# Finishing the last 128 rows of a prefix sum in blocks of 32 rows, with TensorE weighing columns directly

## The chip, the cores and the metric

One NeuronCore of a Trainium2 chip. The metric is the device time of one execution in microseconds. The profile's span (first to last instruction) is some 1.7 us shorter than that time. "Clock" is the share of full speed that the throttle granted TensorE.

## The reference

```python
def setup_inputs():
    B, H, W = 4, 4224, 4224
    return {"x": np.random.randn(B, H, W).astype(np.float32)}

def reference(x):
    ps = np.cumsum(np.cumsum(x, axis=1), axis=2)
    diag = np.diagonal(ps, axis1=1, axis2=2)
    return np.cumsum(diag, axis=1).astype(np.float32)
```

Every output place needs the sum of x over a growing square, so all 285 MB of x must be read once, and the work on it is sums of rows, sums of columns and running sums along 4224 places.

## The kernel before: the parts that matter here

It reads x in strips of 768 rows, cast to bf16 by the DMA, and sums columns on TensorE and rows on ScalarE and VectorE. Apart from a small set-up step at the start, only the end of the last batch is touched by the change. There the last 384 rows come as an upper part (two blocks of 128 rows, `part_a`) and the last 128 rows (`part_b`), each in pieces of columns. The row sums of each are weighted and added to the last 384 output places.

```python
acuts = [(1536, N - HC), (0, 1536)]              # upper blocks, two pieces of columns
bcuts = [(2432, TB), (640, 2432), (0, 640)]      # last 128 rows, three pieces
... # loads on the gpsimd queue; the other places are finished by two scans
fold_in(fold_a, part_a, c0, cp, 256)             # TensorE folds part of the columns
for h in range(2):
    act_sum(asum[:, h, 3:4], part_a[:, h, cp:c1])    # ScalarE sums the others
row_sums(asum[:, :, 4], fold_a)
row_sums(arows, asum)
shares = [(768, 512), (768, 512), (0, 320)]
for i, ((c0, c1), (wp, wa)) in enumerate(zip(bcuts, shares)):
    fold_in(fold_b, part_b, c0, c0 + wp, 256, start=i == 0)
    act_sum(tsum[:, n : n + 1], part_b[:, c0 + wp : c0 + wp + wa])
    if i == 2:
        row_sums(tsum[:, n + 2 : n + 3], fold_b)
    row_sums(tsum[:, n + 1 : n + 2], part_b[:, c0 + wp + wa : c1])
    n += 2
    ... # after piece 0: the products of arows into fin_b and fin_a
row_sums(ttot, tsum)                             # one total per row
matmul(fin_b, ttot, weights[:, 0:P])             # weights: row r counts for places >= r
for fin, c0, c1 in ((fin_a, 0, 2 * P), (fin_b, 2 * P, GW)):
    nc.vector.tensor_add(out=yl[:, c0:c1], in0=fin, in1=c12[0:1, 1, c0:c1])
    nc.sync.dma_start(out=out[b, T0 + c0 : T0 + c1].unsqueeze(0), in_=yl[:, c0:c1])
```

## Time and profile before

| | before |
|---|---|
| time, median of the first 3 runs | 669.03 us (668.8 to 669.93) |
| span of the trace | 667.0 us |
| DMA engines busy | 90% or more in 39 of 40 slices |
| first use of the second upper piece, on ScalarE | 658.53 us |
| end of the last sums | 664.08 us |
| end of the last addition | 665.05 us |

The prediction below shows the profile's lines for these. Each line of the order of instructions gives the start and the length in us, the engine, the source line, the operation, and what it writes and reads. A bracket at the end is the idle time before it and what ended it. In the table of stretches, the columns are busy time (and count) of each engine, then the clock, the DMA share and GB/s.

### The profile page before, as it was taken

How to read it: one execution, taken by the hardware profiler on the slowest of the kernel's cores; microseconds unless marked ns; L12 is line 12 of the kernel's file. 1: busy time of each engine (PE TensorE's matmuls, PEld its weight loads, DVE VectorE, ACT ScalarE, POOL GpSimd, SP SyncE). 2: the span in 40 equal slices, each digit the busy share in tenths (PEclk: the TensorE clock that was granted, in tenths of full speed). 3: DMA queues.
4: the chain of work that ended last, by engine and by line, in shares of the span. 5: the costliest groups of instructions: out<-in, count | busy, mean ns of one | idle time of the engine just before them, and what ended most of it. 6: DMA issues, size and time to landing. Idle time of an engine off the chain costs nothing.

```text
span 667.0 us, 2828 instructions
## 1 busy us (share of the span) xinstructions
PE 215.1 (32%) x967; PEld 97.2 (15%) x967; DVE 336.3 (50%) x376; ACT 140.1 (21%) x225; POOL 27.0 (4%) x56
## 2 busy tenths in 40 slices
PE   0071522403118254140321633504032254250426
PEld 0030211101003022010110311201011122120202
DVE  2043617366924351745883415266398241635687
ACT  0001120406300103040630020304063002030436
POOL 5000000000000000000000000000000000001000
PEclk9995857666558586665655957567565586765758
DMA  9999999999999999999999999999999999999997
GB/s 203 219 219 219 218 219 219 217 217 216 208 215 219 219 219 217 216 219 219 219 219 215 216 211 217 220 219 216 216 216 219 220 215 218 216 215 219 216 207 144
DMA packets 7384, 143.25 MB, mean 215 GB/s; under 512 B 669, under 2 KB 842, under 8 KB 1866
## 3 DMA queue, kind: packets, MB, share of 16 engines
q0 software_dynamic: 7008, 142.47, 99.7%
q1 hardware_dynamic: 362, 0.61, 0.3%
q8 instruction: 7, 0.11, 0.1%
q14 instruction: 7, 0.06, 0.0%
HBM read 285.47 MB, written 0.07 MB: 428 GB/s over the span
## 4 chain that ended last, share of the span: by engine, by line
another core or an unknown queue 42%; DVE 25%; PE 23%; DMA 5%; issue 4%; DVEq 0%; POOLq 0%
PE d L198 23%; DVE acc L215 17%; DVE mu L218 7%; DMA strip<-in_x_dram 5%; PE fold L198 1%; DVE pu L215 0%; DVE c L397 0%; DVE c L218 0%; DVE tsum L215 0%; DVE acc L301 0%; DVE acc L304 0%; PE carry_ps L198 0%; DVE rows L331 0%; DVEq L218 0%
## 5 line engine op out<-in xcount | busy, mean ns | idle before, releaser
L218 DVE SCALAR_TENSOR_TENSOR mu<-strip,um 128x768 bf16<-128x768 bf16 (+1 forms) x129 | 110.7, 908 | 314.4 <-DMA strip<-in_x_dram 222.3
L198 PE MATMUL d<-strip,sel 128*11 128x384 bf16 x603 | 140.0, 406 | 344.4 <-DMA strip<-in_x_dram 344.4
L210 ACT ACTIVATE dump<-strip 128x416 bf16<-128x416 bf16 (+8 forms) x112 | 128.4, 1146 | 523.2 <-DMA strip<-in_x_dram 520.2
L215 DVE TENSOR_REDUCE acc<-strip 128x6 f32<-128x4608 bf16 (+6 forms) x23 | 195.9, 8518 | 0.0
L198 PEld LDWEIGHTS <-sel 128*11 128x11 bf16 x849 | 86.1, 101 | 526.3 <-issue 488.4
L198 PE MATMUL d<-mu,sel 128*11 128x384 bf16 x243 | 59.7, 355 | 67.5 <-DVE mu L218 67.4
L75 POOL DMA_DIRECT2D strip<-in_x_dram x24 | 16.5, 687 | 555.5 <-DVE acc L215 414.5
L210 ACT ACTIVATION_READ_ACCUMULATOR dump<-strip 128x1 f32 x112 | 20.9, 186 | 0.0
L218 DVE DVE_READ_ACCUMULATOR mu<-strip,um 128x1 f32 x129 | 10.6, 82 | 0.0
L198 PE MATMUL d<-ident,rows 128*11 128x128 f32 x24 | 5.2, 378 | 16.5 <-DVE rows L340 16.5
L198 PE MATMUL fold<-strip,ident_h 128*128 128x480 bf16 (+1 forms) x14 | 4.3, 458 | 8.4 <-DMA strip<-in_x_dram 8.4
L198 PE MATMUL d<-halves,rows 128*11 128x64 f32 x48 | 5.7, 304 | 0.0
L198 PEld LDWEIGHTS d<-halves,rows 128*11 128x11 f32 x48 | 5.1, 136 | 2.1 <-issue 2.1
L198 PEld LDWEIGHTS d<-ident,rows 128*11 128x11 f32 x24 | 2.6, 118 | 18.2 <-DVE rows L340 11.5
L215 DVE TENSOR_REDUCE pu<-d 11x1 f32<-11x384 f32 x4 | 2.2, 546 | 5.5 <-PE d L198 5.5
L397 DVE TENSOR_TENSOR_SCAN c<-ones_row,carry,c 11x384 f32<-11x384 f32 x4 | 4.0, 1006 | 0.1
L397 DVE TENSOR_TENSOR_SCAN c<-ones_row,carry,d 11x384 f32<-11x384 f32 x4 | 4.0, 1001 | 0.1
L198 PEld LDWEIGHTS <-ident_h 128*128 128x128 bf16 x20 | 2.2, 112 | 12.2 <-issue 11.8
L215 DVE TENSOR_REDUCE parts<-strip 128x3 f32<-128x3072 bf16 x1 | 3.4, 3350 | 0.0
L198 PE MATMUL d<-hmu,sel 128*11 128x384 bf16 (+2 forms) x3 | 0.7, 286 | 6.7 <-DVE hmu L218 6.7
L372 POOL DMA_DIRECT2D strip<-in_x_dram x2 | 1.4, 716 | 29.2 <-DVE acc L215 29.2
L215 DVE TENSOR_REDUCE tsum<-strip 128x1 f32<-128x384 bf16 (+2 forms) x3 | 1.7, 568 | 0.9 <-DMA strip<-in_x_dram 0.9
(78 smaller groups left out, 36.0 us busy)
## 6 DMA issues: line engine op xcount, KB each, us to landing
strip<-in_x_dram POOLq DMA_DIRECT2D x19, 6336.0 KB, 69.6
strip<-in_x_dram POOLq DMA_DIRECT2D x5, 3168.0 KB, 55.3
strip<-in_x_dram POOLq DMA_DIRECT2D x1, 1080.0 KB, 45.3
strip<-in_x_dram POOLq DMA_DIRECT2D x1, 768.0 KB, 48.2
head<-in_x_dram SPq DMA_DIRECT2D x1, 528.0 KB, 3.9
strip<-in_x_dram POOLq DMA_DIRECT2D x1, 448.0 KB, 51.1
strip<-in_x_dram POOLq DMA_DIRECT2D x1, 416.0 KB, 49.5
strip<-in_x_dram POOLq DMA_DIRECT2D x1, 160.0 KB, 51.4
```

What stands on the lines that cost most here:

```text
L75: nc.gpsimd.dma_start(out=o, in_=x[b, r0 : r0 + f * P, :].rearrange("(p f) w -> p f w", f=f))
L198: nc.tensor.matmul(o, lhsT=lhsT, rhs=rhs, start=start, stop=False, skip_group_check=True)
L210: nc.scalar.activation(out=dump[:, :w], in_=src, func=ACT.Copy, accum_out=acc)
L215: nc.vector.reduce_sum(out=acc, in_=src, axis=AX.X)
L218: nc.vector.scalar_tensor_tensor(out=o, in0=i, scalar=1.0, in1=m, op0=ALU.mult, op1=ALU.mult, accum_out=acc,)
L372: nc.gpsimd.dma_start(out=part_a[:, :, c0:c1], in_=src_a[:, :, c0:c1])
L397: nc.vector.tensor_tensor_scan(out=c12[:, i, :], data0=ones_row, data1=src, initial=carry[:, i : i + 1], op0=ALU.mult, op1=ALU.add,)
```

## The change

Its intent: after the last byte has landed, do less in series. The last 128 rows come as four blocks of 32 rows, and each row is spread over four partitions (128 partitions per block), the last block in two pieces. Blocks 0 and half of 1 are multiplied by TensorE with the place weights (`weights4`, each row's weight repeated four times). Their columns then only need adding up, which a product with a column of ones does. ScalarE and VectorE sum the rest, and every partial sum goes through its own product at once instead of through a total. The last 32 rows reach only the last 32 places, so these are finished apart from the others.

```diff
+    matmul(w4_ps, quarter, weights[:R, :P], start=True)      # set-up; R = 32
+    weights4 ... weights4_h ... ones_col ...
-            bcuts = [(2432, TB), (640, 2432), (0, 640)]
+            for sb, c0, c1 in ((0, 0, CB), (1, 0, CB), (2, 0, CB), (3, 0, bcut), (3, bcut, CB)):
+                r0 = TB + sb * R                                # CB = 1024, bcut = 640
+                nc.gpsimd.dma_start(out=part_b[:, sb, c0:c1],
+                    in_=x[b, r0 : r0 + R, :TB].rearrange("r (k c) -> r k c", k=4)[:, :, c0:c1])
-            fold_in(fold_a, part_a, c0, cp, 256, start=True)
+            fold_in(fold_a, part_a, c0, cp, P, start=True)
...
-        ttot = last.tile([P, 1], FP32, name="ttot")
-        row_sums(ttot, tsum)
-        matmul(fin_b, ttot, weights[:, 0:P])
+        for sb, cp in ((0, CB), (1, c1a)):                     # c1a = CB // 2
+            for c in range(0, cp, P):
+                matmul(by_ps[:, sb * R :], part_b[:, sb, c : c + P],
+                    weights4_h[:, : P - sb * R], start=sb == 0 and c == 0)
+        act_sum(bsum[:, 0:1], part_b[:, 1, c1a:])
+        nc.scalar.copy(out=by, in_=by_ps)
+        fins = ((fin_a, 0, M0), (fin_m, M0, E0), (fin_e, E0, GW))   # 256, 96, 32 places
+        ... # products of arows, of the diagonal, of bsum, and of ones_col with by
+        finish(fin_a, 0, M0)
+        act_sum(bsum[:, 1:2], part_b[:, 2, : CB // 2])
+        row_sums(bsum[:, 2:3], part_b[:, 2, CB // 2 :])
+        for k in (1, 2):
+            weigh(bsum[:, k : k + 1], weights4, M0 + 2 * R, fins)
+        for k, (c0, cm, c1) in enumerate(((0, 320, bcut), (bcut, bcut + 128, CB))):
+            act_sum(esum[:, 2 * k : 2 * k + 1], part_b[:, 3, c0:cm])
+            row_sums(esum[:, 2 * k + 1 : 2 * k + 2], part_b[:, 3, cm:c1])
+        for k in range(4):
+            weigh(esum[:, k : k + 1], weights4, E0, fins)       # only fin_e is reached
+        finish(fin_m, M0, E0)                                   # then out[.. : T0 + E0]
+        finish(fin_e, E0, GW)                                   # then the last 32 places
```

More of the change, by code (lines that the diff above doesn't have):

```diff
@@ L192 @@
     )
+    R = P // 4
+    quarter = consts.tile([R, P], FP32, name="quarter")
+    nc.gpsimd.memset(quarter, 1.0)
+    for base, step in ((0, 1), (3, -1)):
+        nc.gpsimd.affine_select(
+            out=quarter,
+            in_=quarter,
+            compare_op=ALU.is_ge,
+            fill=0.0,
+            base=base,
+            pattern=[[step, P]],
+            channel_multiplier=-4 * step,
+        )
     ident_h = consts.tile([P, P], BF16, name="ident_h")
@@ L200, in matmul @@
         )
+    w4_ps = psum_s.tile([P, P], FP32, name="fold")
+    matmul(w4_ps, quarter, weights[:R, :P], start=True)
+    weights4 = consts.tile([P, P], FP32, name="weights4")
+    nc.vector.tensor_copy(out=weights4, in_=w4_ps)
+    weights4_h = consts.tile([P, P], BF16, name="weights4_h")
+    nc.vector.tensor_copy(out=weights4_h, in_=w4_ps)
+    ones_col = consts.tile([P, 1], FP32, name="ones_col")
+    nc.vector.memset(ones_col, 1.0)
     def fold_in(o, src, c0, c1, w, start=False):
@@ L242 @@
     asum = last.tile([P, 2, 5], FP32, name="asum")
-    tsum = last.tile([P, 8], FP32, name="tsum")
+    dtot = last.tile([P, 1], FP32, name="dtot")
     hs = last.tile([P, 3], FP32, name="hs")
@@ L320 @@
                 masked(hmu[:, 2, :P], diag_b, um1[:, :P], hu[:, 2:3])
-                nc.vector.tensor_sub(
-                    out=tsum[:, 0:1], in0=hs[:, 2:3], in1=hu[:, 2:3]
-                )
+                nc.vector.tensor_sub(out=dtot, in0=hs[:, 2:3], in1=hu[:, 2:3])
                 for h in range(3):
@@ L368 @@
             part_a = strip[:, 0:2]
-            part_b = strip[:, 2]
+            part_b = strip[:, 2, :TB].rearrange("p (s c) -> p s c", s=4)
             acuts = [(1536, N - HC), (0, 1536)]
@@ L372 @@
                 nc.gpsimd.dma_start(out=part_a[:, :, c0:c1], in_=src_a[:, :, c0:c1])
-            bcuts = [(2432, TB), (640, 2432), (0, 640)]
-            for c0, c1 in bcuts:
-                nc.gpsimd.dma_start(out=part_b[:, c0:c1], in_=x[b, TB:N, c0:c1])
-            fold_a = psum_s.tile([P, 2, 256], FP32, name="fold_a")
+            CB = TB // 4
+            bcut = 640
+            for sb, c0, c1 in (
+                (0, 0, CB),
+                (1, 0, CB),
+                (2, 0, CB),
+                (3, 0, bcut),
+                (3, bcut, CB),
+            ):
+                r0 = TB + sb * R
+                nc.gpsimd.dma_start(
+                    out=part_b[:, sb, c0:c1],
+                    in_=x[b, r0 : r0 + R, :TB].rearrange("r (k c) -> r k c", k=4)[
+                        :, :, c0:c1
+                    ],
+                )
+            fold_a = psum_s.tile([P, 2, P], FP32, name="fold_a")
             c0, c1 = acuts[0]
             cp, ca = c0 + 768, c0 + 768 + 1152
-            fold_in(fold_a, part_a, c0, cp, 256, start=True)
+            fold_in(fold_a, part_a, c0, cp, P, start=True)
             for h in range(2):
@@ L415 @@
         cp = c0 + 768
-        fold_in(fold_a, part_a, c0, cp, 256)
+        fold_in(fold_a, part_a, c0, cp, P)
         for h in range(2):
@@ L421, with weigh, finish @@
         row_sums(arows, asum)
-        fold_b = psum_s.tile([P, 256], FP32, name="fold")
-        fin_a = psum_s.tile([1, 2 * P], FP32, name="fin_a")
-        fin_b = psum_s.tile([1, P], FP32, name="fin_b")
-        shares = [(768, 512), (768, 512), (0, 320)]
-        n = 1
-        for i, ((c0, c1), (wp, wa)) in enumerate(zip(bcuts, shares)):
-            fold_in(fold_b, part_b, c0, c0 + wp, 256, start=i == 0)
-            act_sum(tsum[:, n : n + 1], part_b[:, c0 + wp : c0 + wp + wa])
-            if i == 2:
-                row_sums(tsum[:, n + 2 : n + 3], fold_b)
-            row_sums(tsum[:, n + 1 : n + 2], part_b[:, c0 + wp + wa : c1])
-            n += 2
-            if i == 0:
-                matmul(fin_b, arows[:, 0:1], weights[:, 2 * P : GW], start=True)
-                matmul(fin_b, arows[:, 1:2], weights[:, P : 2 * P])
-                matmul(fin_a, arows[:, 0:1], weights[:, 0 : 2 * P], start=True)
-                matmul(fin_a[:, P : 2 * P], arows[:, 1:2], weights[:, 0:P])
-        ttot = last.tile([P, 1], FP32, name="ttot")
-        row_sums(ttot, tsum)
-        matmul(fin_b, ttot, weights[:, 0:P])
-        yl = last.tile([1, GW], FP32, name="yl")
-        for fin, c0, c1 in ((fin_a, 0, 2 * P), (fin_b, 2 * P, GW)):
+        M0 = 2 * P
+        E0 = GW - R
+        fin_a = psum_s.tile([1, M0], FP32, name="fin_a")
+        fin_m = psum_s.tile([1, E0 - M0], FP32, name="fin_m")
+        fin_e = psum_s.tile([1, R], FP32, name="fin_e")
+        yl = last.tile([1, GW], FP32, name="yl")
+        def weigh(rows, w, r0, fins, start=False):
+            for fin, f0, f1 in fins:
+                g0 = max(f0, r0)
+                if g0 < f1:
+                    matmul(
+                        fin[:, g0 - f0 :], rows, w[:, g0 - r0 : f1 - r0], start=start
+                    )
+        def finish(fin, c0, c1):
             nc.vector.tensor_add(
@@ L448 @@
             )
-            nc.sync.dma_start(
-                out=out[b, T0 + c0 : T0 + c1].unsqueeze(0), in_=yl[:, c0:c1]
-            )
+        by_ps = psum_s.tile([P, P], FP32, name="fold")
+        c1a = CB // 2
+        for sb, cp in ((0, CB), (1, c1a)):
+            for c in range(0, cp, P):
+                matmul(
+                    by_ps[:, sb * R :],
+                    part_b[:, sb, c : c + P],
+                    weights4_h[:, : P - sb * R],
+                    start=sb == 0 and c == 0,
+                )
+        bsum = last.tile([P, 3], FP32, name="bsum")
+        act_sum(bsum[:, 0:1], part_b[:, 1, c1a:])
+        by = last.tile([P, P], FP32, name="by")
+        nc.scalar.copy(out=by, in_=by_ps)
+        fins = ((fin_a, 0, M0), (fin_m, M0, E0), (fin_e, E0, GW))
+        weigh(arows[:, 0:1], weights, 0, fins[:1], start=True)
+        weigh(arows[:, 1:2], weights, P, fins[:1])
+        weigh(arows[:, 0:1], weights, 0, fins[1:], start=True)
+        weigh(arows[:, 1:2], weights, P, fins[1:])
+        weigh(dtot, weights, M0, fins)
+        weigh(bsum[:, 0:1], weights4, M0 + R, fins)
+        weigh(ones_col, by, M0, fins)
+        finish(fin_a, 0, M0)
[3 more added lines that the diff above has]
+            weigh(bsum[:, k : k + 1], weights4, M0 + 2 * R, fins)
+        esum = last.tile([P, 4], FP32, name="esum")
+        for k, (c0, cm, c1) in enumerate(((0, 320, bcut), (bcut, bcut + 128, CB))):
[4 more added lines that the diff above has]
+        finish(fin_m, M0, E0)
+        nc.sync.dma_start(
+            out=out[b, T0 : T0 + E0].unsqueeze(0), in_=yl[:, :E0]
+        )
+        finish(fin_e, E0, GW)
+        nc.sync.dma_start(out=out[b, T0 + E0 : N].unsqueeze(0), in_=yl[:, E0:])
 _INS = ['x']
```

## The prediction

> **What bounds the kernel now.** I read the page's strip of 40 slices first, then the queues, then the stretches of the tail one by one, and at last the order of instructions in the final 4 us. The slices and queues:
>
> ```profile
> DVE  2043617366924351745883415266398241635687
> PEclk9995857666558586665655957567565586765758
> DMA  9999999999999999999999999999999999999997
> GB/s 203 219 219 219 218 219 219 217 217 216 208 215 219 219 219 217 216 219 219 219 219 215 216 211 217 220 219 216 216 216 219 220 215 218 216 215 219 216 207 144
> ...
> q0 software_dynamic: 7008, 142.47, 99.7%
> ```
>
> The 16 DMA engines are 90% busy or more in 39 of 40 slices, at 215 to 220 GB/s (bytes as written in bf16; twice that is read). No compute engine is above 50% of the span. So the kernel is as long as reading x takes, plus a head of about 1 us and a tail after the last bytes. The change alters neither bytes nor the order of the large loads; it works only on the tail. How long is that tail? Stretches of the last microseconds (columns: stretch, its length, PE, weight loads, DVE, ACT, POOL, then clock, DMA share, GB/s):
>
> ```profile
> 656.50:658.50 2.00, 1.17 (x10) 0.48 (x9) 1.34 (x5) 0.90 (x2) 0.00 (x0) 1.00 1.07 211
> 658.50:660.50 2.00, 0.81 (x4) 0.29 (x4) 1.96 (x3) 1.87 (x4) 0.00 (x0) 1.00 1.07 211
> 660.50:662.60 2.10, 1.71 (x11) 0.85 (x11) 1.08 (x3) 0.72 (x2) 0.00 (x0) 1.00 0.63 116
> 662.60:663.50 0.90, 0.50 (x4) 0.23 (x3) 0.88 (x2) 0.72 (x2) 0.00 (x0) 1.00 0.04 7
> 663.50:665.30 1.80, 0.38 (x2) 0.09 (x2) 1.29 (x5) 0.56 (x2) 0.00 (x0) 1.00 0.00 0
> 665.30:667.00 1.70, 0.00 (x0) 0.00 (x0) 0.00 (x0) 0.00 (x0) 0.00 (x0) 0.66 0.00 1
> ```
>
> Transfers run full until about 661, thin out as the engines finish unevenly, and are over at about 663.3. From 663.5 to 665.3 only compute is left, then 1.7 us in which only the output's write is under way. The order of work in that end (start, duration, engine):
>
> ```profile
> 662.62 0.69 DVE L215 TENSOR_REDUCE tsum<-strip 128x1 f32<-128x512 bf16 x1 [0.94 <-DMA strip<-in_x_dram]
> ...
> 663.22 0.41 DVE L215 TENSOR_REDUCE tsum<-fold 128x1 f32<-128x256 f32 x1
> 663.51 0.47 ACT L210 ACTIVATE dump<-strip 128x320 bf16<-128x320 bf16 x1
> 663.55 0.47 DVE L215 TENSOR_REDUCE tsum<-strip 128x1 f32<-128x320 bf16 x1
> 663.89 0.19 ACT L210 ACTIVATION_READ_ACCUMULATOR dump<-strip 128x1 f32 x1
> 664.13 0.16 DVE L215 TENSOR_REDUCE ttot<-tsum 128x1 f32<-128x8 f32 x1
> 664.21 0.40 DVE L446 TENSOR_TENSOR yl<-fin_a,c 1x256 f32<-1x256 f32 x1
> 664.35 0.09 PEld L198 LDWEIGHTS fin_b<-weights,ttot 128*1 128x1 f32 x2 [1.50 <-DVE ttot L215]
> 664.35 0.38 PE L198 MATMUL fin_b<-weights,ttot 128*1 128x128 f32 x2 [1.22 <-DVE ttot L215]
> 664.64 0.66 SPq L449 DMA_DIRECT2D out_dram<-yl  x2
> 664.77 0.28 DVE L446 TENSOR_TENSOR yl<-fin_b,c 1x128 f32<-1x128 f32 x1 [0.16 <-PE fin_b L198]
> ```
>
> ScalarE begins the third piece at 663.51, 0.08 us after it was free, so I put that piece's landing at 663.47. The pieces before it were first used at 660.49 (416 KB) and 662.62 (448 KB), so the three land 2.03, 2.13 and 0.85 us apart, counting from the upper block at 658.49. After the landing: sums until 664.02, total until 664.29, matmul until 664.73, addition until 665.05, write until 667.0. That is 3.5 us, of which 1.6 us is compute. Only those 1.6 us, a quarter of one per cent, are on offer.
>
> **What the Trainium skill says.** [...] last addition done at 665.05, end at 667.0, 1.95 us, which the change cannot shorten. (2) "VectorE: DVE Perf Modes", section "The perf-mode tier table", allows tensor_reduce only the 1x mode in every type. The trace agrees: 686 ns for 512 columns and 474 for 320 give 1.10 ns a column, so 256 columns are about 0.40 us. (3) "ScalarE: Activation LUTs", section "What ACT_TABLE_LOAD costs", gives 186 ns + 0.833 ns a column with immediate operands; the trace has 629 ns for 512 and 469 for 320, the same slope. The next section lists copy as filler in every table set, so the new ScalarE copy should load no table; no run yet shows it. (4) "TensorE: Matmul & The Clock Gate", section "Back-to-back issue gap", has about 81 ns per pair of weight load and 128-column matmul in a full stream. The trace has no such bf16 pair; its 256-column ones with fresh weights start some 0.15 us apart (three in 0.49 us, the last 0.27 long, so two gaps of 0.11; I take 0.12 for 128).
>
> **The change part by part.**
>
> *Setup.* A memset and two selects on POOL after `weights` (10.28 to 10.79), each 0.1 to 0.2 us as its 11x11 selects show; one fp32 matmul; two copies and a memset on DVE, which now waits for POOL until about 12 us before sums that used to end at 8.8. The first strip lands at 34.6 us. About 20 us of slack: cost 0.
>
> *Loads.* The same 2 MB of x, as 256, 256, 256, 160 and 96 KB in bf16 instead of 416, 448 and 160. POOL issues them at 611 at about 0.6 us each, 50 us ahead: two more issues cost 0. On the queue, the first two old pieces ran at 205 to 210 KB per us, so 160 KB should have taken 0.77 us and took 0.85: some 0.08 us extra for a short piece. With two more pieces the last byte's signal comes about 0.13 us later, at 663.6. Landings: 659.75, 661.05, 662.3, 663.1, 663.6.
>
> *Upper blocks.* The fold of 768 columns by 256 becomes one by 128: six matmuls of 256 elements instead of three of 512, perhaps 0.2 us more on PE while it waits for DVE anyway, and the reduction of the fold falls from 0.66 to about 0.41 us (256 elements). `arows` is ready near 660.9 instead of 661.22. Not on the final path.
>
> *Blocks 0 and 1.* Eight plus four weighted matmuls replace the folds: 8 x 0.12 = 1.0 us inside the wait for block 1, then 4 x 0.12, done at about 661.65. ScalarE sums half of block 1 (0.75 us with its read) and copies the 128x128 product (about 0.3 us by the slope above) by 662.1. TensorE then owes fin_a (0.64 us between starts in the trace) and small fp32 pairs. From the trace a pass of 128 columns takes 0.107 us and passes of 1 or 2 columns start 0.02 us apart, so 96 columns cost 0.08 and 32 about 0.03: the two upper blocks 4 x 0.11 = 0.44, diagonal 0.22, block 1 0.16, product 0.22, block 2 0.22; with fin_a 1.9 us, from 661.65 to 663.55. That still precedes the last sums.
>
> *Last block.* ScalarE: 512 columns of block 2 from 662.3, 320 of piece one from 663.1 (0.60 to the next), 128 of piece two from 663.7, read at 664.1. VectorE: addition of fin_a 0.40 until 662.7, 512 columns until 663.3, 320 until 663.65, then 256 columns (0.40) until 664.0. The step `ttot` (0.16 plus 0.11 around it) is gone: each partial sum goes to PE itself. After 664.1: two pairs of 32 columns, about 0.16 us latency, ready at 664.4; addition of 32 places 0.19 (402 ns for 256, 279 for 128, 0.96 ns a place) until 664.65. Addition of fin_m (0.25) goes before it, in PE's shadow. The first output (352 places) is issued near 664.2 for 0.23 us, so SyncE is free for the second.
>
> *Sum on the path after the landing*: sums to 664.1 against 664.02 (+0.08, of which the landing is 0.13), total -0.27, matmul -0.14, addition -0.09: 664.65 against 665.05, so **-0.4 us**. Then the same 1.95 us. 669.03 - 0.4 = **668.6 us**.
>
> **The rivals.**
>
> 1. *TensorE becomes the bound.* It now has over 40 small fp32 passes in order behind block 1. If a pass costs 0.1 us whatever its width, as the weight loads' own 0.08 us hints, the list ends about 1.5 us later, near 665, and the last four esum products wait behind it: about +0.5 us, 669.5. Against it: the carry matmuls' starts 0.02 us apart. This is the rival I fear most.
> 2. *The loads get slower.* Five pieces in runs of 4 KB instead of 6.6 or 7 KB. If each piece cost 0.3 us extra, or the new row order spread unevenly over the 16 DMA engines, landing would move by 0.5 to 1 us: 669.2 to 669.7. For it: the unevenness between 661 and 663.3; against: the same bytes, still 128 partitions.
> 3. *The write hides or eats the gain.* A last write of 128 bytes in place of 512 could take longer, or queue behind the first. Then the gain is nil: 669.0.
> 4. *ScalarE is late.* A table load for the copy (1.28 us at the start of the trace) would push 664.1 past 665: 669.6.
>
> **Range and chances.** All of these move the time by 1 us or less, and 2% is 13.4 us. The three runs before spread from 668.8 to 669.93, more than the effect. So the range is mostly the scatter of the median: 667.7 to 669.7. Chances: faster by over 2% 0.01, within 2% 0.98, slower 0.01.
>
> **What would show it right or wrong.** Right: first use of the last piece 3.0 to 3.2 us before the end instead of 3.5; no idle DVE or ACT between the last two pieces; fin_e's last product starting within 0.1 us of ScalarE's last read; last addition near 0.19 us; the slices of DMA unchanged. Wrong in step: products of bsum still running when the last sums are ready (rival 1); gaps between pieces above 1.4 us for 256 KB (rival 2); over 2.1 us from the last addition to the end (rival 3); a table load in the tail (rival 4). The whole prediction falls if any early strip moves, for the argument takes the first 655 us as unchanged.

## The result

| | before | after |
|---|---|---|
| median, 6 runs each, same rounds | 669.29 us (668.8 to 669.93) | 668.62 us (668.22 to 669.49) |
| span of the trace | 667.0 us | 666.5 us |
| T: ScalarE's first use of the second upper piece to the end of the span | 8.47 us | 8.08 us |
| L: end of the last sums to the end of the last addition | 0.97 us | 0.55 us |

The ratio is 0.9992 with a 95% interval of 0.9979 to 1.0005, which makes the two the same at 2%. A ratio compares runs of the two kernels in the same rounds, so it is not quite the ratio of the medians.

T and L are lengths inside one trace. They are counted from events of the tail, whenever the data of the first 655 us arrived, so they carry most of the argument. Most of the expectations quoted below count T from TensorE's first use of that piece, which is 0.03 to 0.05 us earlier (8.51 before, 8.12 after); the last one counts from ScalarE's, as the table does.

The stretches of the tail after the change, with the same bounds as those of before:

```profile
660.50:662.60 2.10, 1.72 (x23) 1.33 (x24) 0.62 (x3) 1.28 (x4) 0.00 (x0) 1.00 0.87 151
662.60:663.50 0.90, 0.77 (x18) 0.55 (x14) 0.90 (x3) 0.83 (x4) 0.00 (x0) 1.00 0.05 8
663.50:665.30 1.80, 0.56 (x8) 0.29 (x8) 0.66 (x3) 0.46 (x3) 0.00 (x0) 1.00 0.00 1
```

The transfers still thin out and end near 663.3. In the stretch after them, VectorE is busy 0.66 us instead of 1.29. The order of instructions at the end, for the changed kernel:

```profile
662.00 0.41 DVE L477 TENSOR_TENSOR yl<-fin_a,c 1x256 f32<-1x256 f32 x1 [1.48 <-PE fin_a L214]
...
662.93 0.89 DVE L240 TENSOR_REDUCE esum<-strip 128x1 f32<-128x320 bf16 x2
...
662.99 0.47 ACT L235 ACTIVATE dump<-strip 128x320 bf16<-128x320 bf16 x1
...
663.59 0.31 ACT L235 ACTIVATE dump<-strip 128x128 bf16<-128x128 bf16 x1
...
663.61 0.28 PE L214 MATMUL fin_e<-weights,esum 128*1 128x32 f32 x4 [0.24 <-ACT dump L235]
663.75 0.23 DVE L477 TENSOR_TENSOR yl<-fin_m,c 1x96 f32<-1x96 f32 x1
663.80 0.19 ACT L235 ACTIVATION_READ_ACCUMULATOR dump<-strip 128x1 f32 x1
664.01 0.23 SPq L522 DMA_DIRECT2D out_dram<-yl  x1
...
664.04 0.28 PE L214 MATMUL fin_e<-weights,esum 128*1 128x32 f32 x4 [0.16 <-ACT dump L235]
664.36 0.18 DVE L477 TENSOR_TENSOR yl<-fin_e,c 1x32 f32<-1x32 f32 x1 [0.38 <-PE fin_e L214]
```

Against the lines of before: the last sum ends at 664.00 instead of 664.08, but nothing stands between it and the product. The product takes 0.28 us instead of 0.38, the addition 0.18 instead of 0.28, and the last addition ends at 664.54 instead of 665.05. TensorE waits for ScalarE before both pairs of esum products, so it isn't the bound. From block 2 on ScalarE goes from piece to piece without waiting for data, and it ends last. VectorE lost 1.48 us waiting for fin_a earlier. From the last addition to the end it is 1.96 us (1.95 before).

### The profile page after: what moved, and what is told of

It reads as the page before. It is cut to its first block, busy times and chain, and to the rows that moved or that the text cites. A ratio compares the mean times of both kernels' runs of the same rounds, so it can differ in the third digit from the quotient of the medians.

```text
span 666.5 us, 2923 instructions
## 1 busy us (share of the span) xinstructions
PE 214.0 (32%) x1011; PEld 99.1 (15%) x1011; DVE 336.1 (50%) x378; ACT 140.6 (21%) x228; POOL 28.0 (4%) x61
## 4 chain that ended last, share of the span: by engine, by line
another core or an unknown queue 38%; DVE 24%; PE 21%; DMA 13%; issue 4%; ACT 0%; POOL 0%; DVEq 0%; ACTq 0%; POOLq 0%
PE d L214 21%; DVE acc L240 16%; DMA strip<-in_x_dram 13%; DVE mu L243 6%; ACT dump L235 0%; DVE pu L240 0%; DVE c L243 0%; POOL strip L395 0%; DVE acc L329 0%; DVE acc L326 0%; PE carry_ps L214 0%; DVE rows L354 0%; DVEq L243 0%; DVE rows L363 0%
## 5 line engine op out<-in xcount | busy, mean ns | idle before, releaser
L214 PE MATMUL d<-strip,sel 128*11 128x384 bf16 x603 | 138.5, 403 | 334.2 <-DMA strip<-in_x_dram 334.2
L235 ACT ACTIVATE dump<-strip 128x416 bf16<-128x416 bf16 (+9 forms) x113 | 128.7, 1139 | 522.5 <-DMA strip<-in_x_dram 519.7
L214 PE MATMUL fold<-strip,ident_h 128*128 128x480 bf16 x8 | 3.4, 598 | 7.6 <-DMA strip<-in_x_dram 7.6
## 6 DMA issues: line engine op xcount, KB each, us to landing
strip<-in_x_dram POOLq DMA_DIRECT2D x1, 160.0 KB, 43.5
strip<-in_x_dram POOLq DMA_DIRECT2D x1, 96.0 KB, 28.6
```

The costliest lines, as they stand in the source:

```text
L214: nc.tensor.matmul(o, lhsT=lhsT, rhs=rhs, start=start, stop=False, skip_group_check=True)
L235: nc.scalar.activation(out=dump[:, :w], in_=src, func=ACT.Copy, accum_out=acc)
```

## The experiments

The theory: the gain is the shorter chain after the last sums, about 0.4 us, and nothing else. The rivals: TensorE's long list of narrow products eats it; the loads move; the 0.4 us is noise.

**Both kernels again, unaltered.** No edit.

> The kernel before, unaltered, to see how far two traces of one kernel differ. Two lengths are read in every trace: T, from the first use of the second piece of the upper blocks to the end of the span (before 8.51 us, after 8.12), and L, from the end of the last sums on ScalarE or VectorE to the end of the last addition (before 664.08 to 665.05 = 0.97 us, after 664.00 to 664.54 = 0.54). Theory (a shorter chain after the last byte, and nothing else): T 8.4 to 8.6, L 0.97 within 0.03. If T itself varies by 0.4 us or more, the 0.39 us between the two traces on hand is noise.

> The changed kernel, unaltered, five rounds. Theory: L 0.54 within 0.03, T 8.0 to 8.25; time ratio 0.9994 and not resolved from 1 with some ten runs, since single runs spread over 1.3 us. Rival (the gain in the two traces is noise): T as in the kernel before, about 8.5.

Measured: the changed kernel again has T 8.07, L 0.55, and a median of 668.42 us (668.28 to 669.9). Its ratio to the kernel before of these rounds is 0.9982 (0.9970 to 0.9995). The kernel before has L 1.02, but T is 9.33 and not 8.47, and its four runs lie at 671.03 to 671.19 us; against the other runs of the same code on the same chip, the ratio is 1.0018 (1.0005 to 1.0032). So an interval that leaves out 1 does not show that two kernels differ here: two builds of one kernel are as far apart. This trace differs in two ways. First, the second upper piece was first used at 660.17 instead of 658.53. Second, the clock fell in the middle of the tail. By the letter of the first expectation, a T that varies by 0.4 us or more makes the 0.39 us noise, and T varied by 0.86. But this variation has a cause of its own, shown next, and the traces without a fall stand apart: the kernel before has T 8.47, and 8.54 in the run below that holds the clock up; the changed kernel has 8.08 and 8.07, and 8.10 and 8.11 in two runs below. L separates them in every trace: 0.97 to 1.02 in the four with the old end (this kernel twice, its five-piece form and the warmed one), with and without a fall, and 0.54 to 0.55 in the changed kernel's two and those two runs below. Stretches of this trace of the kernel before:

```profile
655.00:656.00 1.00, 1.00 (x6) 0.46 (x4) 1.00 (x2) 1.00 (x2) 0.00 (x0) 0.66 1.07 213
656.00:662.00 6.00, 3.51 (x30) 1.90 (x28) 5.05 (x12) 4.38 (x9) 0.00 (x0) 1.00 1.04 202
662.00:663.00 1.00, 0.91 (x6) 0.49 (x6) 0.77 (x3) 0.80 (x3) 0.00 (x0) 0.75 0.42 80
663.00:665.00 2.00, 2.00 (x9) 0.73 (x8) 0.69 (x1) 0.71 (x2) 0.00 (x0) 0.50 0.11 20
665.00:666.00 1.00, 0.60 (x3) 0.12 (x1) 0.36 (x2) 0.58 (x3) 0.00 (x0) 0.54 0.00 0
```

The clock (third number from the right) is 1.00 from 656 to 662, then 0.50 from about 662.5 to 665.9, which is 3.4 us. What that does, in the order of instructions of the same trace:

```profile
663.37 1.48 PE L199 MATMUL fin_a<-weights,arows 128*1 128x256 f32 x4
...
664.78 0.82 PE L199 MATMUL fold<-strip,ident_h 128*128 128x256 bf16 x3
...
665.64 0.42 DVE L216 TENSOR_REDUCE tsum<-fold 128x1 f32<-128x256 f32 x1 [0.72 <-PE fold L199]
```

fin_a takes 1.48 us instead of 0.81, the fold behind it starts 0.55 us after VectorE had its share of the same piece, and VectorE waits 0.72 us for it. The prediction had taken a clock of 1.00 for granted.

**The total put back.**

```diff
-        for k in range(4):
-            weigh(esum[:, k : k + 1], weights4, E0, fins)
         finish(fin_m, M0, E0)
+        row_sums(etot, esum)
+        weigh(etot, weights4, E0, fins)
```

> The changed kernel, with the one step back that it removed: the four partial sums of the last block are added up by VectorE, and one product follows instead of four. Theory: the reduction costs what it did before (0.16 us plus 0.11 around it), less the second pair of products that is no longer needed (about 0.07): L 0.70 to 0.80, T 8.3. Rival (the four products on TensorE cost as much as the total did, the gain comes from the narrower end): L 0.54, T 8.1.

Measured: L 0.68, T 8.23, clock 1.00; 668.96 us (0.9988, 0.9972 to 1.0003). The lines of this trace that replace the last pair of products:

```profile
664.26 0.16 DVE L240 TENSOR_REDUCE etot<-esum 128x1 f32<-128x4 f32 x1
664.47 0.22 PE L214 MATMUL fin_e<-weights,etot 128*1 128x32 f32 x2 [0.85 <-DVE etot L240]
664.73 0.18 DVE L477 TENSOR_TENSOR yl<-fin_e,c 1x32 f32<-1x32 f32 x1 [0.31 <-PE fin_e L214]
```

The step comes back with its 0.16 us. The wait from the last sum to the product is 0.24 us instead of 0.05, but one product in 0.22 us now does what two did in 0.28. So L rises by 0.13 and T by 0.15, just under what was expected. The rival (the four products cost as much as the total) would have left T at 8.08. So of the 0.39 us, about 0.15 belongs to the total given up, with products this narrow.

**The last 128 places finished together.**

```diff
-        fins = ((fin_a, 0, M0), (fin_m, M0, E0), (fin_e, E0, GW))
+        fins = ((fin_a, 0, M0), (fin_b, M0, GW))
...
-        finish(fin_m, M0, E0) ... finish(fin_e, E0, GW)
+        finish(fin_b, M0, GW)      # and the first output is then that of fin_a alone
```

> The changed kernel, with the last 128 places finished together, by one 128-wide product and one 128-wide addition, and no middle part. Theory: products of 128 columns cost 0.107 us a pass instead of 0.03, four passes after the last sums, and the addition 0.28 instead of 0.18: L 0.54 + 0.2 + 0.1 = 0.8 to 0.9, T 8.4; so nearly the whole gain would be gone. Rival (the width does not matter, latency does): L below 0.65.

Measured: L 0.59, T 8.67; 668.7 us (0.9987, 0.9972 to 1.0002). My expectation of L was wrong, and the edit shows why: the products of the last block still write only the 32 places from E0 on, so their width did not change. Only the addition did (0.28 us). T is not comparable, because in this trace the clock fell to 0.50 (fin_a took 1.44 us). The narrow product comes from the blocks of 32 rows, then, not from the separate end. The separate end itself is worth the difference of the additions at most, 0.1 us.

**The total given up in the kernel before, alone.**

```diff
-        row_sums(ttot, tsum)
-        matmul(fin_b, ttot, weights[:, 0:P])
+        for k in (0, 1, 2, 3, 4, 6, 5, 7):
+            matmul(fin_b, tsum[:, k : k + 1], weights[:, 0:P])
```

> The kernel before, with one part of the change alone: no total on VectorE, each of the eight partial sums goes through the 128-wide product itself; all but the last two can run before the last sums end. They are written after them in program order but wait only for their own sums. Theory: the total's 0.27 us go, one more 128-wide product (two passes of 0.107) comes on top of the one there was: L 0.97 - 0.27 + 0.2 = 0.85 to 0.95. So this part alone gives about 0.1 us; it pays only with narrow products. Rival (the total alone is the gain): L 0.65 to 0.72.

Measured: L 1.24, T 8.74, clock 1.00; 669.54 us (1.0003, 0.9988 to 1.0018). Both views were wrong: the tail got longer by 0.27 us. The reason is in the order of instructions of this trace:

```profile
664.43 1.91 PE L198 MATMUL fin_b<-weights,tsum 128*1 128x128 f32 x16
...
666.37 0.28 DVE L445 TENSOR_TENSOR yl<-fin_b,c 1x128 f32<-1x128 f32 x1 [0.65 <-PE fin_b L198]
```

Sixteen passes of 128 columns take 1.91 us. They stand in TensorE's order behind the fold of the second piece (until 664.5), so they can't run far enough ahead, as I had assumed: only some ten of the sixteen had started when the last sums ended at 665.41, and VectorE now waits 0.65 us for the rest. This is the prediction's first rival come true, in the kernel before: a partial sum may go straight to TensorE only if its product is narrow. A product is two passes here, and in the changed kernel the four passes over 32 columns that follow the last sums, two products, take 0.28 us. The parts of the change depend on each other.

**Five pieces in the kernel before.**

```diff
-            for c0, c1 in bcuts:
+            for c0, c1 in [(3264, TB), (2432, 3264), (1536, 2432), (640, 1536), (0, 640)]:
```

> The kernel before, with the same columns and sums, but the last rows loaded in five pieces (208, 208, 224, 224, 160 KB) instead of three (416, 448, 160). It measures what two more pieces cost. The prediction: 0.08 us a short piece, so the first use of the last piece 0.13 to 0.16 us later after the first use of the second upper piece (before 5.02 us), T 8.65. Rival (the queue does not notice): 4.9 to 5.05. Rival (each piece costs 0.3 us): 5.6.

Measured: from ScalarE's first use of the second upper piece to that of the last piece 5.03 us (4.98 in the trace on hand, 4.92 in the repeated one). Two more pieces cost 0.05 to 0.11 us, less than the predicted 0.13. Counted from TensorE's first use, as the expectation does, it is 5.08 us, between the theory (5.15 to 5.18) and the rival that the queue does not notice (up to 5.05), so this one trace doesn't decide between these two; it does rule out 0.3 us a piece. T is 9.28, because the clock fell here too; that is as long as the other trace of the kernel before with a fall (9.33). 670.35 us (1.0012, 0.9992 to 1.0032).

**More work for TensorE.** Two, then ten products with a zero column:

```diff
... # zero_col is set up like ones_col
         weigh(ones_col, by, M0, fins)
+        for _ in range(2):      # or 10
+            weigh(zero_col, by, M0, fins)
```

> The changed kernel with two more products of a zero column with the 128x128 matrix of blocks 0 and 1, right after the real one: eight more narrow fp32 passes on TensorE, about 0.11 us a pair of two widths, 0.22 a product. Theory (TensorE has about 0.5 us of slack before the last sums): L 0.54 and T 8.1, unchanged within 0.1. Rival 1 of the prediction (TensorE is at its limit): T up by 0.45.

> The same with ten such products, 40 passes, 10 x 0.22 = 2.2 us of TensorE. Theory: the gaps of the list hold about 0.5 to 0.8 us (0.24 us before the first esum products, 0.16 before the last, the rest earlier), so the end moves by 1.4 to 1.7 us: T 9.5 to 9.8. If narrow passes cost 0.1 us each, as the rival had it, 4 us more: T above 11.

Measured: with two, T 8.10 and L 0.55 at a clock of 1.00, unchanged. The first rival fails at full clock: TensorE has at least 0.44 us (two products of 0.22) to spare at that place of its list. The runs, 668.49 to 671.9 us, scatter too widely to add to this (1.0013, 0.9989 to 1.0037). With ten, T is 10.73 and the time 672.35 us (1.0045, 1.0030 to 1.0059). That is 1 us more than expected, but the clock fell in this trace and fin_a took 1.44 us, so the list started late. The ten products themselves, back at full clock, took 2.23 us (665.33 to 667.56), as expected. Before them, the product with `by` was issued until 5.66 us after the first use of the second upper piece, against 4.44 in the changed kernel: at half clock the same list is 1.2 us later and the slack is gone.

**The clock held up in the kernel before.**

```diff
... # zero_h is set up
+        for _ in range(4):
+            matmul(fold_a, zero_h, part_a[..., z0 : z0 + 256])
         fold_in(fold_a, part_a, c0, cp, 256)
+        for _ in range(4):
+            matmul(fold_a, zero_h, part_a[..., z0 : z0 + 256])
```

> In four of the ten traces so far the granted TensorE clock fell to 0.50 for some 3 us in the middle of the tail (about 6.6 us after it had risen), and T was longer: 9.37 and 9.33 in the two such traces of the kernel before and its five-piece form, against 8.51. In these traces the upper blocks landed late and TensorE had little to do between 659 and 662. Here the kernel before is kept as it is, but eight products with a zero matrix (0.21 us each, no effect on the sums) fill TensorE's waits around the second upper piece. Theory (the fall follows TensorE's idleness and costs the kernel before 0.8 us whenever it comes): clock 1.00 through the tail, T 8.5 to 8.7, time 0.1 to 0.5 us below the kernel before in the mean and no run above 670.3. Rival (the fall comes at its own time): it is seen in this trace as likely as in the others, and runs scatter as before.

Measured: clock 1.00 through the tail, T 8.54, L 0.97. Five of six runs lie between 668.63 and 668.77 us and one at 670.45; the median is 668.74, and the ratio to the kernel before on the same chip 0.9984 (0.9970 to 0.9998). The mean gained 1.0 us where 0.1 to 0.5 was expected, and one run lies above the bound I had set. Work that does nothing made the kernel before about as fast as the changed one. That fits a fall in part of its runs, but one trace without a fall isn't proof that there was none in the other five, and part of the gain may be early arrival of the data (both below).

**fin_a earlier, shares shifted: a version meant to beat both.**

```diff
+            if sb == 0:      # between the products of blocks 0 and 1
+                weigh(arows[:, 0:1], weights, 0, ((fin_a, 0, M0),), start=True)
+                weigh(arows[:, 1:2], weights, P, ((fin_a, 0, M0),))
...
-        weigh(arows[:, 0:1], weights, 0, fins[:1], start=True)
-        weigh(arows[:, 1:2], weights, P, fins[:1])
...
-        for k, (c0, cm, c1) in enumerate(((0, 320, bcut), (bcut, bcut + 128, CB))):
+        for k, (c0, cm, c1) in enumerate(((0, 192, bcut), (bcut, bcut + 96, CB))):
```

> A version meant to beat both. In the changed kernel VectorE sits idle 1.48 us for the fin_a product, which waits in TensorE's order behind block 1, and its addition then delays VectorE's half of block 2 by 0.14 us; ScalarE ends last, 0.18 us after VectorE. Here the fin_a products go between blocks 0 and 1 (TensorE idle there for 0.63 us), and of the last block VectorE takes 448 and 288 columns, ScalarE 192 and 96. Theory: block 2 begins on both engines at its landing, both end about 5.40 to 5.50 us after the second upper piece instead of 5.61, L 0.54: T 7.95 to 8.05. With a clock fall in the tail, where the late fin_a held VectorE up to 664.43 in the trace with the merged end, less is lost. Rival (landing of the last piece is the limit): T 8.1, no gain.

Measured: T 7.94, L 0.49; 668.49 us (0.9980, 0.9966 to 0.9994). In this trace, the addition of fin_a and the sum of block 2:

```profile
661.90 0.41 DVE L477 TENSOR_TENSOR yl<-fin_a,c 1x256 f32<-1x256 f32 x1 [0.90 <-PE fin_a L214]
...
662.48 0.69 DVE L240 TENSOR_REDUCE bsum<-strip 128x1 f32<-128x512 bf16 x1 [0.16 <-DMA strip<-in_x_dram]
```

VectorE now waits for the data of block 2 and no longer for itself, and the tail is 0.14 us shorter than that of the changed kernel, as expected. In time, it cannot be told from the changed kernel (668.62 and 668.42).

**The same with the clock held up.** Twelve products of a zero matrix with 256 elements around the fold, as in the kernel before.

> The same, with twelve narrow products with a zero matrix (256 elements, 0.11 to 0.15 us each) in TensorE's waits around the second upper piece, so that the clock stays at 1.00. Theory: T 7.95 to 8.1 with the clock at 1.00 throughout; scatter of the runs smaller than that of the version without; mean 0.1 to 0.4 us lower. Rival: as without.

Measured: clock 1.00, T 8.01, although the second upper piece was first used as late as 659.99. But the runs spread from 668.26 to 669.93 us (median 669.7; 0.9988, 0.9974 to 1.0001), hardly narrower than without (668.24 to 670.0), so the rival holds for the scatter. This trace had no fall, and its 668.0 us come from late data alone.

**TensorE cold in the changed kernel's tail.** Seven of eight fold products of the strip before are left out, so the sums are wrong on purpose.

```diff
-            fold_in(fold_g, strip[:, F:], 0, wp, 160, start=True)
+            fold_in(fold_g, strip[:, F:], 0, 160, 160, start=True)
```

> The changed kernel with seven of the eight fold products of the strip before the tail left out (so its result is wrong on purpose), to leave TensorE idle from 650 on and hold its granted clock at 0.50 in the tail, in which no trace of the changed kernel itself has had a fall. Theory (at half clock TensorE becomes the bound of the changed kernel's tail too, as the prediction's first rival had it for full clock): measured from ScalarE's first use of the second upper piece, fin_a takes 1.4 to 1.5 us instead of 0.81, VectorE's half of block 2 begins late, the last sums end at 6.1 instead of 5.57, the end comes at 8.6 to 9.3 instead of 8.08 (the kernel before: 9.33 with a fall, 8.47 without). Rival (the narrow products have slack enough at half clock too): end at 8.1 to 8.2. If the clock rises all the same, the run tells nothing of this.

Measured: inconclusive, as the expectation allowed. The clock was 0.50 until about 660.4, just after the first use of the second upper piece at 660.09, and then 1.00: T 8.11, L 0.55; 669.89 us (0.9999, 0.9985 to 1.0013). It shows only that in this trace a low clock up to that moment cost the tail nothing. (The comparison with the reference accepted this result, so its tolerance does not see 1120 columns missing from three row sums a partition.)

## Why the prediction was right

The time came out at 668.62 us for a predicted 668.6. The runs of one kernel spread over more than 1 us, so the closeness to 0.02 us is luck. The steps are what counts, and T checks them without that scatter: -0.4 us predicted, -0.39 and -0.40 measured in the two traces of the changed kernel, against the one trace of the kernel before that is unaltered and has no fall. Of the 0.39, L gives 0.42; the last sums end 0.03 us later after the second upper piece than before (5.58 against 5.55), and the write takes 0.01 more.

- **What bounds the kernel.** Right: the chain after the last landing is all that moved. Nothing in the traces connects the change to the arrival of the data.
- **Set-up.** Right: VectorE ends it at 14.72 us and then waits 20.2 us for the first strip.
- **Loads.** The first uses of the five pieces, counted from TensorE's first use of the second upper piece, were predicted 1.26, 2.56, 3.81, 4.61 and 5.11 us later. The trace has 1.24, 2.50 and 3.82 for the blocks. For the last block it gives only bounds, since both engines were still busy: at most 4.6 and 5.0. The page's list of DMA issues gives more: issued at 619.39 and 634.80 and landed 43.5 and 28.6 us later, so at 662.9 and 663.4 (predicted 663.1 and 663.6). The old last piece, issued at 612.00, landed 51.4 us later, at 663.4 too. (The prediction had all five issued in a row from 611 on; POOL issued the last two later, which cost nothing.) Two more pieces cost 0.05 to 0.11 us, not 0.13. So the second rival fails.
- **Weighted products on TensorE.** Mis-sized: 0.12 us each was taken, but eight span 0.62 us with the last one 0.22 long, so they start 0.057 us apart. The prediction's own lines hinted at it: three products of 256 columns in 0.49 us, the last 0.27 long, start 0.11 us apart, and not 0.15 as it says too, yet it took 0.12 for half as many columns. (Those three also use the same weights, so they say nothing of fresh ones.) The list ended near 663.37 instead of 663.55, still before the last sums. Two additional products fit in without moving the end.
- **ScalarE copy.** 0.25 us, and no table load, so the fourth rival fails.
- **Last sums.** ScalarE ended at 664.00 (664.1 predicted), VectorE at 663.82 (664.0). The prediction misread where they ended before: 664.02 is VectorE, but ScalarE's read in its own lines ends at 664.08 (663.89 + 0.19).
- **After the last sums.** 0.55 us predicted (664.1 to 664.65), 0.54 to 0.55 measured. The split of the gain was less clear than the prediction wrote it: putting the total back costs 0.15 us and not 0.27, because some 0.05 us from the last sum to the product stays in any case, and without the total two products follow the last sums instead of one (0.28 us against 0.22). Finishing the last places alone can be worth 0.1 at most.
- **Write of the output.** 1.95 us before, 1.96 after: 128 bytes take as long as 512, and the first write did not hold up the second. The third rival fails.
- **What was missing.** The prediction took the scatter of runs as given. It has two parts. The first use of the second upper piece lies at 658.42 to 658.76 in seven traces and at 659.67 to 660.17 in the other seven, the kernel before being in both groups. The two groups are already apart by the strip that is first used near 65 us (64.3 to 65.7 against 66.6 to 66.9), that is, long before the tail. Even the first 5 us tell them apart: the DMA engines moved 189 GB/s in all seven early traces and 179 to 184 in the seven late ones. And in four of the seven late traces, never in an early one, the clock fell before the last addition, which made T of the kernel before 9.33, and of its five-piece form 9.28, instead of 8.47.

When does the clock fall? The traces answer more than the experiments asked. Each stretch of one clock in them (the first and the last, which the trace cuts off, aside) is a whole number of windows of 3.41 us, so from a rise one can count where the windows end. At 1.00, over the fourteen traces in full, the clock held after 430 windows, in each of which TensorE was busy 1.83 us or more, and fell after 281, in each of which it was busy 1.87 us or less. In the tail of both traces of the kernel before, one such window lies at about 659.1 to 662.5. First the trace without a fall, then the one with it:

```profile
659.10:662.50 3.40, 1.82 (x12) 0.80 (x10) 2.44 (x5) 2.02 (x6) 0.00 (x0) 1.00 0.83 157
659.10:662.50 3.40, 1.42 (x10) 0.68 (x10) 2.99 (x6) 2.24 (x5) 0.00 (x0) 1.00 0.94 182
```

The third number is TensorE's busy time. The kernel before kept its clock by very little; with late data, less of TensorE's work lies before the window's end. In the other three traces with a fall the window before it had 1.37 to 1.72 us. In the warmed kernel before, the window that ends at 660.04 has 2.96 us, and 1.36 without the zero products, so in this trace they are what kept the fall away. The early traces of the changed kernel and its forms have 2.0 us or more in the windows that end in the tail, but in two of the late ones (the merged end and the ten products) it was 1.72 and the clock fell, so the changed kernel isn't safe from a fall either.

Is the changed kernel faster in time? Over all runs of both (five groups of rounds on several chips, so no paired comparison), the kernel before has 46 runs from 668.69 to 671.34 us with a mean of 669.85. The changed one has 11 runs from 668.22 to 669.9 with a mean of 668.74. That is 1.1 us, more than the 0.39 of the chain. The rest may be a tail that suffers less from a fall: the version with the merged end, close to the changed kernel, had T 8.67 with a fall, against 9.33. No trace of the unaltered changed kernel has a fall, and its two builds may just have been lucky in their data's arrival. So the chain's 0.4 us is shown; the other 0.7 us is only argued. What makes data arrive early or late stays open.

## What to carry to other kernels

In this kernel, bound by its loads, what this change shortened was the chain from the last byte to the last write. Count it in one trace, from a fixed event to the end, since the scatter of the time hides it, and put TensorE's clock into the estimate of any tail in which TensorE mostly waits. Removing a step that joins partial sums pays only if what takes its place is narrow and doesn't queue behind other work: the same removal lengthened the tail of the kernel before by 0.27 us.

## What the Trainium skill lacked or had wrong

- "TensorE: Matmul & The Clock Gate", section "Back-to-back issue gap": about 81 ns per weight load and 128-column matmul in a full stream. Here eight such bf16 pairs, each with new 128x128 weights, started 57 ns apart ((0.62 - 0.22) / 7) at a clock of 1.00, close to the 56 ns that the section gives without new weights.
- No page that I found times an fp32 matmul by its width. Here an fp32 matmul shows as two passes, and sixteen passes of 128 columns took 1.91 us, while four passes of 32 columns took 0.28 us and eight of 32 columns after each other 0.40 us.
- "TensorE: Matmul & The Clock Gate", section "What's actually happening", has a free-running window of about 3.4 us, and the fall lasted 3.4 us (662.5 to 665.9), in agreement. It gives the throttle after an idle window. Here the clock fell although TensorE was busy 1.42 us in the 3.4 us before the fall (659.1 to 662.5), so a window need not be idle for that. The share that decided was some 1.85 of 3.41 us: no fall after 430 windows with 1.83 us or more, a fall after 281 with 1.87 us or less.
- "DMA: Bandwidth & Descriptors", section "Anatomy of one DMA — SWDGE (gpsimd) path", fits about 2.0 us of fixed cost to DMAs issued by gpsimd and has no such total for those that SyncE issues, like the output here. From the last addition to the end it is 1.95 to 2.02 us in all fourteen traces, with SyncE's issue of 0.23 us or more in it.
- I found no page that tells that two builds of one kernel can get their data 1.6 us apart (658.53 against 660.17), which begins to show in the first 5 us.
